# The joint down stage of a DiT block: a normal and a seven-product pair interleaved block by block, and an eighth pair with seven products

## The chip, the cores and the metric

One NeuronCore of one Trainium2 chip runs the whole program in one launch. The metric is the device time of that launch in microseconds; lower is better. A core has engines that run their own instruction streams: TensorE (PE, with its weight loads PEld), VectorE (DVE), ScalarE (ACT), GpSimd (POOL) and SyncE (SP, which here only issues DMAs). They wait for one another by semaphores.

## The reference, cut to what matters

```python
D_MODEL = 2048; SEQ = 256
D_FF = 256 * ((8 * D_MODEL // 3 + 255) // 256)          # 5632
...
def conv_ffn(h, w_up, conv_w, conv_b, w_down):
    a, u = jnp.split(h @ w_up, 2, axis=-1)
    return (jax.nn.silu(depthwise_conv(a, conv_w, conv_b)) * u) @ w_down
...
        ffn_x = conv_ffn(modulate(x_mid, norm2_g[l], mod_x[:, 3], mod_x[:, 4]), w_up[l], conv_w[l], conv_b[l], w_down[l])
        new_x = x_mid + mod_x[:, 5][:, None, :] * ffn_x
```

Everything is float32. The change touches only the last product, `(...) @ w_down`: 256 tokens by 5632 features times 5632 by 2048.

## The kernel before

A float32 product is made of three matmuls in float32r (`mm3`, line 71): both operands are split into a high part (`hi`, a rounded copy) and a low part (`lo`, the rest), and hi·hi, hi·lo and lo·hi are added up in PSUM. The activations are split once when they are made. The weights come from HBM as 128x1024 tiles (`raw`), and for each tile ACT writes `whi` (a cast, line 143) and DVE writes `wlo` (a subtraction, line 144). `chunk` does that for one tile of the down stage, and `fetch` is its DMA, issued by SP. The pools have four buffers of `raw`, two of `araw`, and three of `whi` and of `wlo`. So the cast of a tile can start only when TensorE has finished with the tile three places ahead of it in program order.

The features are 44 tiles of 128. The gated activations of the first 32 are kept (`g0`, `g1`), and `down_two` multiplies them in one joint stage; the last twelve follow later. The joint stage works in two halves of 1024 output columns (`half`, called twice), and each half walks over 16 pairs of feature tiles. A pair is a 2x2 by 2x2 block product: two feature tiles by two token tiles on one side, two feature tiles by two blocks of 512 columns on the other. A **normal** pair takes eight products of 128x512, in two weight tiles: the rows w21, w22 (`nb` below) and then w11, w12 (`na`). A **seven-product** pair takes Winograd's form with seven products. It needs sums of weights and of activations: weight tile `sb` (w21, w22) gives two products, `sa` (its half w11) one, `t` (two sums, made by `two` on DVE into `araw`) two, and `f` (two more sums, by `four`) two. The sums of activations (s1, s2, s4) are made by `seven_acts` while the up stage runs, and kept in the tiles `sa` and `sb` of SBUF. Each of these groups is one `chunk`, with a cast and a subtraction of its own. Seven pairs, the odd ones up to 13, are of the second kind (`SEVEN`).

Pair follows pair: block i is pair 2i, normal (nb, na), then pair 2i+1 with seven products (sb, sa, t, f). Pairs 14 and 15 are both normal. In each half four PSUM banks (`norm`) take the normal products and some of the seven, and four (`sev`) the rest of them. After the last seven-product pair (line 1003) five instructions combine the `sev` banks into `y`, and at the end of the half four more add the `norm` banks (line 1013). In the second half `before()` calls `turn` (line 1015) after the first pair: 16 transposes on TensorE of the first half's `y`, and eight additions into `xm` on DVE.

Instructions are written in program order, but a scheduler puts each engine's list in an order by priority, and `chunk` raises the priority of its loads and splits, so that they stand ahead of the products that use them. Each engine then runs its own list strictly in that order.

Of the kernel before, what the change touches and what calls it, by code (L numbers as in the profile page):

```python
# [35 lines left out]
SEVEN = (1, 3, 5, 7, 9, 11, 13)  # L36
# [15 lines left out]
def block_kernel(ctx, tc, xct, prm, cst, ada2, wst, out):  # L52
# [895 lines left out]
    def half(n, g0, g1, norm, sev, y, before):  # L948
# [5 lines left out]
        def add(b, a, w, start=False, stop=False):  # L954
            mm3(b, *a, *w, start, stop)
        first = SEVEN[0]
        for p in range(16):
            k1, k2 = 2 * p, 2 * p + 1
            rb, (w21, w22) = chunk(2, fetch)
            a11, a21, a12, a22 = act(k1, 0), act(k1, 1), act(k2, 0), act(k2, 1)  # L960
            if p not in SEVEN:
                st0, sp = p == 0, p == 15
                if sp:
                    ra, (w11, w12) = chunk(2, fetch)
                    for b, u1, u2, v1, v2 in ((0, a11, a12, w11, w21), (1, a11, a12, w12, w22), (2, a21, a22, w11, w21),
                                              (3, a21, a22, w12, w22)):
                        add(norm[b], u1, v1)
                        add(norm[b], u2, v2, stop=True)
                    break
                add(norm[0], a12, w21, st0)  # L970
                add(norm[2], a22, w21, st0)
                add(norm[1], a12, w22, st0)
                add(norm[3], a22, w22, st0)
                ra, (w11, w12) = chunk(2, fetch)
                add(norm[0], a11, w11)
                add(norm[2], a21, w11)
                add(norm[1], a11, w12)
                add(norm[3], a21, w12)
                if p == 0:
                    before()  # L980
                continue
            f, l = p == first, p == SEVEN[-1]
            d = sums[p]
            s1, s2, s4 = [(d[:, 0, i * P:i * P + P], d[:, 1, i * P:i * P + P]) for i in range(3)]
# [9 lines left out]
            add(sev[1], s1, t1, f, l)  # L994
            add(sev[3], a21, t3, f, l)
# [5 lines left out]
            add(sev[2], s2, t2, f, l)  # L1001
# [225 lines left out]
```

## Time and profile before

| | us |
|---|---|
| median of 3 runs | 1675.78 |
| lowest and highest of them | 1674.80 and 1676.34 |
| the profiled execution, device time | 1675.59 |
| the profiled execution, span from first to last instruction | 1673.8 |
| joint down stage, from its first matmul (1295.89) to the first of the next up stage (1468.41) | 172.52 |
| granted clock of TensorE, mean | 1.00 |

The profile is of one execution, and its times are counted from the first instruction. A matmul of 128x512 is listed with 0.39 us, but matmuls overlap, so the distance between two starts tells the rate. In a row of the timeline, what stands in brackets is the time for which the engine stood idle ahead of the instruction, and whose work ended that.

### The profile page before, as it was taken

How to read it: one execution, taken by the hardware profiler on the slowest of the kernel's cores; microseconds unless marked ns; L12 is line 12 of the kernel's file. 1: busy time of each engine (PE TensorE's matmuls, PEld its weight loads, DVE VectorE, ACT ScalarE, POOL GpSimd, SP SyncE). 2: the span in 40 equal slices, each digit the busy share in tenths (PEclk: the TensorE clock that was granted, in tenths of full speed). 3: DMA queues.
4: the chain of work that ended last, by engine and by line, in shares of the span. 5: the costliest groups of instructions: out<-in, count | busy, mean ns of one | idle time of the engine just before them, and what ended most of it. 6: DMA issues, size and time to landing. Idle time of an engine off the chain costs nothing.

```text
span 1673.8 us, 25069 instructions
## 1 busy us (share of the span) xinstructions
PE 1660.3 (99%) x9508; PEld 1392.2 (83%) x9508; DVE 1264.6 (76%) x2014; ACT 862.1 (52%) x1323; POOL 68.3 (4%) x132
## 2 busy tenths in 40 slices
PE   8999999999999999999999999999999999999999
PEld 3668888888888888888888988888888777788887
DVE  3448985666879886878879887788767888866665
ACT  4337542433646764554455665555555555545542
POOL 0000100000000000001100000000000000000000
PEclk9999999999999999999999999999999999999999
DMA  9997834534466657878856577677555565655554
GB/s 378 408 356 246 286 122 158 178 111 154 162 216 211 214 202 277 285 242 280 285 202 234 182 247 256 212 273 252 191 183 190 185 212 187 201 183 192 187 199 149
DMA packets 104153, 371.85 MB, mean 222 GB/s; under 512 B 11488, under 2 KB 13920, under 8 KB 104032
## 3 DMA queue, kind: packets, MB, share of 16 engines
q1 hardware_dynamic: 85600, 303.14, 51.3%
q0 software_dynamic: 18432, 67.12, 12.3%
q8 instruction: 74, 1.21, 0.3%
q14 instruction: 47, 0.39, 0.1%
HBM read 368.11 MB, written 2.10 MB: 221 GB/s over the span
## 4 chain that ended last, share of the span: by engine, by line
PE 96%; DMA 2%; DVE 1%; ACT 0%; issue 0%; SPq 0%; DVEq 0%; ACTq 0%
PE bankm L69 85%; PE banks L69 9%; DMA ringv<-in_wst_dram 1%; DMA ringq<-in_wst_dram 1%; PE banks L406 0%; PE banks L610 0%; PE banks L779 0%; PE banks L602 0%; DVE wlo L114 0%; DMA xraw<-in_xct_dram 0%; PE banks L611 0%; PE banks L224 0%; PE banks L632 0%; PE banks L749 0%; PE banks L1022 0%
## 5 line engine op out<-in xcount | busy, mean ns | idle before, releaser
L69 PE MATMUL bankm<-hl,whi 128*128 128x512 f32 (+1 forms) x3136 | 970.4, 392 | 0.0
L114 DVE TENSOR_TENSOR wlo<-raw,whi 128x1024 fp32r<-128x1024 f32 (+2 forms) x434 | 528.1, 1218 | 240.0 <-ACT whi L113 238.2
L113 ACT CAST whi<-raw 128x1024 fp32r<-128x1024 f32 (+2 forms) x434 | 453.2, 1045 | 479.5 <-PE bankm L69 366.4
L69 PEld LDWEIGHTS bankm<-hl,wlo 128*128 128x128 f32 x2848 | 533.2, 188 | 120.6 <-DVE wlo L114 0.4
L69 PE MATMUL bankm<-hl,wlo 128*128 128x256 f32 (+2 forms) x2848 | 610.2, 287 | 0.0
L69 PEld LDWEIGHTS bankm<-hl,whi 128*128 128x128 f32 x3136 | 494.9, 189 | 20.3 <-DVE hl L153 0.4
L69 PE MATMUL bankm<-whi,hl 128*128 128x512 f32 x640 | 209.2, 395 | 1.2 <-ACT hl L245 1.0
L398 DVE SCALAR_TENSOR_TENSOR acc<-araw,csil,acc 128x1024 f32<-128x1024 f32 x120 | 153.4, 1279 | 2.1 <-DMA araw<-in_ada_dram 1.6
L69 PEld LDWEIGHTS bankm<-whi,hl 128*128 128x128 f32 x640 | 119.7, 188 | 28.0 <-ACT hl L245 2.6
L69 PE MATMUL bankm<-wlo,hl 128*128 128x512 f32 x320 | 124.7, 392 | 0.0
L393 POOL DMA_DIRECT2D araw<-in_ada_dram x128 | 68.1, 532 | 1092.2 <-DVE acc L398 566.9
L143 ACT CAST whi<-raw 128x1024 fp32r<-128x1024 f32 x64 | 61.1, 956 | 42.1 <-PE bankm L69 25.4
L69 PE MATMUL bankm<-yb,whi 128*128 128x512 f32 x256 | 80.7, 397 | 0.0
L144 DVE TENSOR_TENSOR wlo<-raw,whi 128x1024 fp32r<-128x1024 f32 x64 | 69.3, 1104 | 2.2 <-ACT whi L143 1.1
L69 PEld LDWEIGHTS bankm<-wlo,hl 128*128 128x128 f32 x320 | 60.1, 188 | 12.9 <-DVE wlo L144 0.4
L69 PEld LDWEIGHTS bankm<-yb,wlo 128*128 128x128 f32 x256 | 48.1, 188 | 11.3
L910 ACT ACTIVATE fs<-fs,prm 128x256 f32<-128x256 f32 x44 | 26.4, 601 | 49.8 <-DVE fs L464 49.8
L69 PE MATMUL bankm<-yb,wlo 128*128 128x256 f32 x256 | 50.6, 279 | 0.0
L143 ACT CAST whi<-araw 128x1024 fp32r<-128x1024 f32 x28 | 29.5, 1054 | 34.3 <-PE banks L69 17.0
L144 DVE TENSOR_TENSOR wlo<-araw,whi 128x1024 fp32r<-128x1024 f32 x28 | 34.3, 1224 | 16.2 <-ACT whi L143 14.5
L69 PE MATMUL bankm<-whi,g 128*128 128x512 f32 x136 | 46.1, 390 | 0.0
L226 DVE TENSOR_REDUCE tn<-banks 128x8 f32<-128x32 f32 (+1 forms) x9 | 1.7, 188 | 53.1 <-ACT whi L113 50.1
(281 smaller groups left out, 1538.9 us busy)
## 6 DMA issues: line engine op xcount, KB each, us to landing
raw<-in_wst_dram SPq DMA_DIRECT2D x489, 512.0 KB, 4.1
araw<-in_ada_dram POOLq DMA_DIRECT2D x128, 512.0 KB, 4.7
ringv<-in_wst_dram SPq DMA_DIRECT2D x24, 512.0 KB, 9.9
ringq<-in_wst_dram SPq DMA_DIRECT2D x20, 512.0 KB, 9.9
araw<-in_wst_dram SPq DMA_DIRECT2D x10, 512.0 KB, 9.9
xraw<-in_xct_dram SPq DMA_DIRECT2D x8, 512.0 KB, 7.3
raw<-in_wst_dram SPq DMA_DIRECT2D x7, 384.0 KB, 9.9
ringkT<-in_wst_dram SPq DMA_DIRECT2D x5, 512.0 KB, 9.9
```

The source lines that it names most:

```text
L69: return PE.matmul(o, l, r, start=start, stop=stop, skip_group_check=True)
L113: S.copy(hi, raw)
L114: self.last = V.tensor_tensor(lo, raw, hi.bitcast(F32), op=ALU.subtract)
L143: S.copy(hi[:, w], raw[:, w])
L144: V.tensor_tensor(lo[:, w], raw[:, w], hi[:, w].bitcast(F32), op=ALU.subtract)
L226: V.tensor_reduce(m8, aps[:, 0:w].rearrange("p (q g c) -> p q c g", q=2 * n, g=4)[:, :, 0:2, :], axis=AX.X, op=ALU.add)
L393: nc.gpsimd.dma_start(raw, ada2[idx])
L398: V.scalar_tensor_tensor(acc, raw, csil[:, kt, 0:1], acc, op0=ALU.mult, op1=ALU.add)
L910: S.activation(t, s, AF.Identity, bias=cb[:, f:f + 1], scale=cw[:, f, 1:2])
```

## The change

`SEVEN` gets pair 15 as an eighth seven-product pair, and `half` is written in eight blocks. Blocks 0 to 6 hold a normal pair 2i and a seven-product pair 2i+1 whose chunks are mixed: sb, nb, sa, t, na, f (in block 0 nb comes first, and `before()` right behind it). Block 7 holds pair 15, then the combination of the `sev` banks, and then pair 14 as the normal pair that closes the half. The weights are laid out in HBM in the new order. The kept sums grow by 3 KB a partition, and the scratch of GpSimd's DMA descriptors is set from 8192 to 4096.

```diff
-SEVEN = (1, 3, 5, 7, 9, 11, 13)
+SEVEN = (1, 3, 5, 7, 9, 11, 13, 15)
...
-            sums["b"] = big.tile([P, 2, 2, 3 * P], F32R, name="sb", tag="sb")
+            sums["b"] = big.tile([P, 3, 2, 3 * P], F32R, name="sb", tag="sb")
...
-        for p in range(16):
...
+        for i in range(8):
+            pn, ps = (2 * i, 2 * i + 1) if i < 7 else (14, 15)
+            st0, last = i == 0, i == 7
...
+            def normal_b():
+                _, (w21, w22) = chunk(2, fetch)
+                for b, x, w in ((0, n12, w21), (2, n22, w21), (1, n12, w22), (3, n22, w22)):
+                    add(norm[b], x, w, st0)
+
+            def normal_a():
+                _, (w11, w12) = chunk(2, fetch)
+                for b, x, w in ((0, n11, w11), (2, n21, w11), (1, n11, w12), (3, n21, w12)):
+                    add(norm[b], x, w)
+
+            if st0:
+                normal_b()
+                before()
             rb, (w21, w22) = chunk(2, fetch)
...
             add(norm[0], a12, w21)
             add(norm[1], s4, w22)
+            if not st0 and not last:
+                normal_b()
             ra, (w11,) = chunk(1, fetch)
-            add(sev[0], a11, w11, f, l)
+            add(sev[0], a11, w11, st0, last)
...
             r2, (t1, t3) = chunk(2, two, "araw")
...
+            if not last:
+                normal_a()
...
             r4, (t2, t4) = chunk(2, four, "araw")
...
+        y12, y34 = y
+        S.copy(y12[:, 0], sev[0])
...
+        _, (w21, w22) = chunk(2, fetch)
+        _, (w11, w12) = chunk(2, fetch)
+        for b, u1, u2, v1, v2 in ((0, n11, n12, w11, w21), (1, n11, n12, w12, w22), (2, n21, n22, w11, w21),
+                                  (3, n21, n22, w12, w22)):
+            add(norm[b], u1, v1)
+            add(norm[b], u2, v2, stop=True)
...
-    nc = bacc.Bacc("TRN2", target_bir_lowering=False, num_devices=1, dynamic_dma_scratch_size=8192)
+    nc = bacc.Bacc("TRN2", target_bir_lowering=False, num_devices=1, dynamic_dma_scratch_size=4096)
```

What the scheduler makes of it is seen in the engines' lists. First TensorE's list before, in block 0 of the first half: `whi_12180` is sb, `whi_12192` is sa and `whi_12201` is t, whose buffer was that of na. The rows stand right behind the last matmul of na and end with the first that needs t's low part.

```order
L69 MATMUL bankm_12134<-whi_12180,hl_88 128x512
L69 MATMUL bankm_12134<-wlo_12181,hl_88 128x512
L69 MATMUL bankm_12134<-whi_12180,hl_88 128x512
L69 MATMUL bankm_12135<-whi_12180,sa_9137 128x512
L69 MATMUL bankm_12135<-wlo_12181,sa_9137 128x512
L69 MATMUL bankm_12135<-whi_12180,sa_9137 128x512
L69 MATMUL bankm_12133<-whi_12192,hl_88 128x512
L69 MATMUL bankm_12133<-wlo_12193,hl_88 128x512
L69 MATMUL bankm_12133<-whi_12192,hl_88 128x512
L69 MATMUL banks_12138<-whi_12201,sa_9137 128x512
L69 MATMUL banks_12140<-whi_12201,hl_88 128x512
L69 MATMUL banks_12138<-wlo_12202,sa_9137 128x512
```

So the twelfth matmul behind na is the first to need t's low part, and the other blocks are alike. The same place of the changed kernel: `whi_12171` is sb, and `whi_12192` is t, whose buffer was that of nb; the rows stand right behind the last matmul of nb.

```order
L69 MATMUL bankm_12143<-whi_12171,hl_88 128x512
L69 MATMUL bankm_12143<-wlo_12172,hl_88 128x512
L69 MATMUL bankm_12143<-whi_12171,hl_88 128x512
L69 MATMUL bankm_12144<-whi_12171,sa_9137 128x512
L69 MATMUL bankm_12144<-wlo_12172,sa_9137 128x512
L69 MATMUL bankm_12144<-whi_12171,sa_9137 128x512
L69 MATMUL banks_12147<-whi_12192,sa_9137 128x512
L69 MATMUL banks_12149<-whi_12192,hl_88 128x512
L69 MATMUL banks_12147<-wlo_12193,sa_9137 128x512
```

In block 0 it is now the ninth. In a later block of the changed kernel (here block 2 of the first half: `whi_12349` is sa, `whi_12358` t, `whi_12371` na) the chunk that takes over the buffer of nb is na, and the rows again stand right behind the last matmul of nb.

```order
L69 MATMUL bankm_12142<-whi_12349,hl_88 128x512
L69 MATMUL bankm_12142<-wlo_12350,hl_88 128x512
L69 MATMUL bankm_12142<-whi_12349,hl_88 128x512
L69 MATMUL banks_12147<-whi_12358,sa_9137 128x512
L69 MATMUL banks_12147<-wlo_12359,sa_9137 128x512
L69 MATMUL banks_12147<-whi_12358,sa_9137 128x512
L69 MATMUL banks_12149<-whi_12358,hl_88 128x512
L69 MATMUL banks_12149<-wlo_12359,hl_88 128x512
L69 MATMUL banks_12149<-whi_12358,hl_88 128x512
L69 MATMUL bankm_12143<-whi_12371,hl_88 128x512
L69 MATMUL bankm_12145<-whi_12371,hl_88 128x512
L69 MATMUL bankm_12143<-wlo_12372,hl_88 128x512
```

There it is the twelfth again, as before, with na in the place of t. The second place is TensorE's list in the second half, right behind the transposes. Before, `whi_12876` is sb, `whi_12888` sa, `whi_12897` t and `whi_12910` f; na stands ahead of the transposes.

```order
L1022 MATMUL bankm_12812<-cst_77,yva_12142 128x128
L69 MATMUL bankm_12805<-whi_12876,hl_88 128x512
L69 MATMUL bankm_12805<-wlo_12877,hl_88 128x512
L69 MATMUL bankm_12805<-whi_12876,hl_88 128x512
L69 MATMUL banks_12806<-whi_12876,sa_9137 128x512
L69 MATMUL banks_12806<-wlo_12877,sa_9137 128x512
L69 MATMUL banks_12806<-whi_12876,sa_9137 128x512
L69 MATMUL bankm_12809<-whi_12888,hl_88 128x512
L69 MATMUL bankm_12809<-wlo_12889,hl_88 128x512
L69 MATMUL bankm_12809<-whi_12888,hl_88 128x512
L69 MATMUL bankm_12810<-whi_12897,sa_9137 128x512
```

Now `whi_12878` is sb and `whi_12912` is na, which takes over the buffer of sb.

```order
L1024 MATMUL bankm_12832<-cst_77,yva_12151 128x128
L69 MATMUL bankm_12825<-whi_12878,hl_88 128x512
L69 MATMUL bankm_12825<-wlo_12879,hl_88 128x512
L69 MATMUL bankm_12825<-whi_12878,hl_88 128x512
L69 MATMUL banks_12826<-whi_12878,sa_9137 128x512
L69 MATMUL banks_12826<-wlo_12879,sa_9137 128x512
L69 MATMUL banks_12826<-whi_12878,sa_9137 128x512
L69 MATMUL bankm_12825<-whi_12912,hl_88 128x512
L69 MATMUL banks_12827<-whi_12912,hl_88 128x512
L69 MATMUL banks_12826<-whi_12912,hl_88 128x512
L69 MATMUL banks_12828<-whi_12912,hl_88 128x512
L69 MATMUL bankm_12825<-wlo_12913,hl_88 128x512
```

No matmul stands any more between the last of sb and the first of the chunk that takes its buffer. The third place is DVE's list in block 3 of the first half. Before, the low parts are those of nb, na and sb, then sa (512 wide), t and f, with the sums in `araw` between them.

```order
L144 TENSOR_TENSOR wlo_12394<-raw_12392,whi_12393 128x1024
L144 TENSOR_TENSOR wlo_12412<-raw_12410,whi_12411 128x1024
L144 TENSOR_TENSOR wlo_12430<-raw_12428,whi_12429 128x1024
L991 TENSOR_TENSOR araw_12449<-raw_12440 128x512
L992 TENSOR_TENSOR araw_12449<-raw_12440,raw_12428 128x512
L144 TENSOR_TENSOR wlo_12442<-raw_12440,whi_12441 128x512
L998 TENSOR_TENSOR araw_12462<-araw_12449,raw_12428 128x512
L999 TENSOR_TENSOR araw_12462<-araw_12462,raw_12428 128x512
L144 TENSOR_TENSOR wlo_12451<-araw_12449,whi_12450 128x1024
L144 TENSOR_TENSOR wlo_12464<-araw_12462,whi_12463 128x1024
```

Now they are sb, then three sums, nb, sa, the fourth sum, t, na and f.

```order
L144 TENSOR_TENSOR wlo_12403<-raw_12401,whi_12402 128x1024
L986 TENSOR_TENSOR araw_12440<-raw_12431 128x512
L987 TENSOR_TENSOR araw_12440<-raw_12431,raw_12401 128x512
L995 TENSOR_TENSOR araw_12471<-araw_12440,raw_12401 128x512
L144 TENSOR_TENSOR wlo_12415<-raw_12413,whi_12414 128x1024
L144 TENSOR_TENSOR wlo_12433<-raw_12431,whi_12432 128x512
L996 TENSOR_TENSOR araw_12471<-araw_12471,raw_12401 128x512
L144 TENSOR_TENSOR wlo_12442<-araw_12440,whi_12441 128x1024
L144 TENSOR_TENSOR wlo_12455<-raw_12453,whi_12454 128x1024
L144 TENSOR_TENSOR wlo_12473<-araw_12471,whi_12472 128x1024
```

The ten instructions of a block are the same in kind and number; three sums now stand between the low parts of sb and of nb.

## Rows read from the trace of the kernel before

**Rows 1.** The page: span, busy time of each engine, and the chain's shares.

```profile
span 1673.8 us, 25069 instructions
...
PE 1660.3 (99%) x9508; PEld 1392.2 (83%) x9508; DVE 1264.6 (76%) x2014; ACT 862.1 (52%) x1323; POOL 68.3 (4%) x132
...
PE 96%; DMA 2%; DVE 1%; ACT 0%; issue 0%; SPq 0%; DVEq 0%; ACTq 0%
```

**Rows 2.** Busy time by windows: length, PE, PEld, DVE, ACT, POOL; clock, DMA.

```profile
1295.89:1314.52 18.63, 18.63 (x82) 14.68 (x80) 15.75 (x22) 11.38 (x16) 0.00 (x0) 1.00 0.54 177
1314.52:1367.05 52.53, 52.53 (x227) 41.36 (x226) 45.27 (x50) 28.98 (x32) 0.00 (x0) 1.00 0.63 203
1367.05:1401.23 34.18, 33.95 (x155) 27.15 (x154) 30.74 (x40) 16.01 (x19) 0.00 (x0) 1.00 0.52 181
1401.23:1453.71 52.48, 52.48 (x226) 41.31 (x226) 45.27 (x50) 28.92 (x32) 0.00 (x0) 1.00 0.62 204
1453.71:1468.41 14.70, 14.70 (x72) 12.05 (x71) 12.54 (x15) 7.45 (x9) 0.00 (x0) 1.00 0.57 193
```

**Rows 3.** Who waited for whom, 1285 to 1480: total us, times, longest.

```profile
ACT whi L143 <- PE bankm L69: 38.4, 38, 3.7
...
PEld bankm L69 <- DVE wlo L144: 2.6, 7, 0.4
PEld banks L69 <- DVE wlo L144: 2.6, 7, 0.4
```

**Rows 4.** Timeline of block 2, first half: start, us, engine, instruction.

```profile
1322.17 0.62 PE L69 MATMUL bankm<-whi,hl 128*128 128x512 f32 x2
...
1322.64 1.05 ACT L143 CAST whi<-araw 128x1024 fp32r<-128x1024 f32 x1 [2.14 <-DVE araw L999]
...
1323.73 2.59 DVE L144 TENSOR_TENSOR wlo<-araw,whi 128x1024 fp32r<-128x1024 f32 x2 [1.15 <-ACT whi L143]
...
1324.67 0.39 PE L69 MATMUL banks<-whi,hl 128*128 128x512 f32 x1
...
1325.01 0.19 PEld L69 LDWEIGHTS banks<-wlo,sa 128*128 128x128 f32 x1 [0.38 <-DVE wlo L144]
...
1325.35 0.40 PE L69 MATMUL banks<-whi,sa 128*128 128x512 f32 x1
```

**Rows 5.** Groups of instructions, 1312 to 1382, shapes apart: busy, mean ns.

```profile
L144 DVE TENSOR_TENSOR wlo<-raw,whi 128x1024 fp32r<-128x1024 f32 x20 | 23.9, 1220 | 1.3 <-ACT whi L143 0.8
L143 ACT CAST whi<-raw 128x1024 fp32r<-128x1024 f32 x22 | 23.0, 1050 | 10.0 <-PE bankm L69 8.8 <-PE banks L69 1.2
...
L999 DVE TENSOR_TENSOR araw<-araw,raw 128x512 f32<-128x512 f32 x6 | 4.1, 692 | 0.2
```

**Rows 6.** Timeline of DVE around the second half's start.

```profile
1369.97 2.35 DVE L144 TENSOR_TENSOR wlo<-raw,whi 128x1024 fp32r<-128x1024 f32 x2
...
1377.33 1.28 DVE L1013 TENSOR_TENSOR ykT<-bankm,ykT 128x512 f32<-128x512 f32 x2
...
1388.60 1.66 DVE L1025 SCALAR_TENSOR_TENSOR xm<-bankm,modv,xm 128x256 f32<-128x256 f32 x4
```

**Rows 7.** Timeline of PE around the second half's start.

```profile
1386.03 0.28 PE L1022 MATMUL bankm<-cst,ykT 128*128 128x128 f32 x1
...
1387.70 0.47 PE L69 MATMUL bankm<-whi,hl 128*128 128x512 f32 x1
...
1390.84 0.39 PE L69 MATMUL banks<-whi,hl 128*128 128x512 f32 x1
1391.46 0.50 PE L69 MATMUL bankm<-whi,hl 128*128 128x512 f32 x1 [0.23 <-ACT whi L143]
1391.79 0.39 PE L69 MATMUL banks<-whi,hl 128*128 128x512 f32 x1
```

**Rows 8.** Instructions that make a pair's sums (min/median/max ns), 980 to 1262.

```profile
L937 DVE TENSOR_TENSOR t<-fs x7: 282/284/292, 990.7 to 1257.7; 128x128 f32<-128x128 f32 x7
...
L153 DVE TENSOR_TENSOR sb<-t,sb x2: 551/552/553, 1214.8 to 1260.3; 128x384 fp32r<-128x384 f32 x2
```

**Rows 9.** What GpSimd's DMA issues waited for, and who waited for them.

```profile
  DVE acc L398: 566.9, 100
...
  DVE acc L398: 1.6, 1
```

More of the change, by code (lines that the diff above doesn't have):

```diff
@@ L955, in add @@
             mm3(b, *a, *w, start, stop)
-        first = SEVEN[0]
-        for p in range(16):
-            k1, k2 = 2 * p, 2 * p + 1
-            rb, (w21, w22) = chunk(2, fetch)
[L960 to L984, printed above, removed]
@@ new lines, in half @@
+        for i in range(8):
+            pn, ps = (2 * i, 2 * i + 1) if i < 7 else (14, 15)
+            st0, last = i == 0, i == 7
+            a11, a21, a12, a22 = act(2 * ps, 0), act(2 * ps, 1), act(2 * ps + 1, 0), act(2 * ps + 1, 1)
+            n11, n21, n12, n22 = act(2 * pn, 0), act(2 * pn, 1), act(2 * pn + 1, 0), act(2 * pn + 1, 1)
+            d = sums[ps]
+            s1, s2, s4 = [(d[:, 0, i * P:i * P + P], d[:, 1, i * P:i * P + P]) for i in range(3)]
+            def normal_b():
[9 more added lines that the diff above has]
+                before()
+            rb, (w21, w22) = chunk(2, fetch)
@@ L993, in half @@
             r2, (t1, t3) = chunk(2, two, "araw")
-            add(sev[1], s1, t1, f, l)
-            add(sev[3], a21, t3, f, l)
+            add(sev[1], s1, t1, st0, last)
+            add(sev[3], a21, t3, st0, last)
+            if not last:
+                normal_a()
             def four(raw):
@@ L1000, in half @@
             r4, (t2, t4) = chunk(2, four, "araw")
[L1001 removed]
+            add(sev[2], s2, t2, st0, last)
             add(norm[2], a22, t4)
[L1003 to L1009 removed]
+        y12, y34 = y
+        S.copy(y12[:, 0], sev[0])
+        V.tensor_tensor(y34[:, 0], sev[2], y12[:, 0], op=ALU.subtract)
+        V.tensor_tensor(y12[:, 1], sev[1], y34[:, 0], op=ALU.add)
+        V.tensor_tensor(y34[:, 0], sev[3], y34[:, 0], op=ALU.add)
+        V.tensor_tensor(y34[:, 1], sev[3], y12[:, 1], op=ALU.add)
+        _, (w21, w22) = chunk(2, fetch)
[4 more added lines that the diff above has]
+            add(norm[b], u2, v2, stop=True)
         with tc.high_priority(offset=RUSH):
@@ L1209, in downs @@
         return np.concatenate([_duos(np, d[:KT - 2]), _halves(np, d[KT - 2:])], 0)
-    pairs = g["w_down"][0].reshape(NFF // 2, 2, P, 2, 1024)[:16, ::-1].transpose(3, 0, 1, 2, 4).reshape(-1, P, 1024)
+    pairs = g["w_down"][0].reshape(NFF // 2, 2, P, 2, 1024)[:16].transpose(3, 0, 1, 2, 4)
+    order = [(0, 1), (1, 1), (1, 0), (0, 0)]
+    for i in range(1, 7):
+        order += [(2 * i + 1, 1), (2 * i, 1), (2 * i + 1, 0), (2 * i, 0)]
+    order += [(15, 1), (15, 0), (14, 1), (14, 0)]
+    pairs = np.stack([pairs[h, p, k] for h in range(2) for p, k in order])
     parts += [ups(0), ups(1), pairs, ups(2), downs(2)]
```

7 lines of the change are left out of this document (removed).

## The prediction

> **What bounds the kernel now.** I read the page first. PE is busy for 99% of the span and holds 96% of the chain [rows 1], so the stage of the change has to be read on PE. The windows over the joint down stage say the same at first sight: in 52.53 us PE is busy for all 52.53, at granted clock 1.00 [rows 2]. But a matmul of 0.39 us overlaps the next, and a short wait disappears in that overlap, so I went from busy time to distances between starts.
>
> In the timeline eleven steps lie between 1322.17 and 1324.67 [rows 4]: 0.2273 us for a matmul of 128x512. The stage holds 726 of them (two halves of 121 products, three matmuls each). Between the window edges stand 80, 225, 138, 225 and 58, since a block of two pairs has 45 and each edge is the same matmul of a block; 16 transposes fall into the third window and 12 into the last, at 0.104 us each (16 in 1386.03 to 1387.70 [rows 7]). What a window has beyond that is waiting: 18.63 − 18.18 = 0.45; 52.53 − 51.14 = 1.39; 34.18 − 31.37 − 1.66 = 1.15; 52.48 − 51.14 = 1.34; 14.70 − 13.18 − 1.25 = 0.27 [rows 2]. Together 4.60 us. Nothing done to waiting can win more here.
>
> What is waited for stands in the next two views. ACT's casts wait for PE to free a buffer, 38.4 us in 38 waits, and PE's weight loads wait for low parts, 14 times and never over 0.4 us [rows 3]. The timeline has one such case step by step [rows 4]: PE starts the last matmul that reads a buffer at 1322.17, the cast into it starts at 1322.64 (+0.47) and takes 1.05, the low part 1.22 [rows 5] (the second of the two merged on DVE at 1323.73), and the weight load of t's low part starts at 1325.01, after 0.38 of waiting. So **from the last use of a buffer to the use of the next low part in it takes 2.84 us**, whatever else goes on; the high part alone is usable after 0.47 + 1.05 + about 0.06 = 1.58. With 12 slots as cover (2.73 us), 0.11 of the 2.84 is left over, and the restart costs 0.11 more, because the weight load is no longer hidden (1325.01 to 1325.35 is 0.34 against 0.227). That is 0.22, and windows 2 and 4 give 1.39/5 = 0.28 and 1.34/5 = 0.27 a block. Thirteen such blocks are about 3.5 of the 4.60 us; the other 1.1 lies mostly around the half boundary.
>
> The repeating gap has a rule in the Trainium skill, page "Perfetto Trace Analysis", section Optimization Strategy: one gap that keeps repeating on the engine that should be full can mean too few buffers for the next tile. The casts that wait for PE, 38.4 us, agree [rows 3].
>
> **The change, part by part.**
>
> *One pair with seven products instead of eight.* In each half three matmuls fewer: 6 × 0.2273 = **−1.36 us**, on the path. The same section's neighbour in the skill, Identifying the Most-Contended Engine, holds matmul busy time to be a poor measure of how near the limit a kernel is and wants the weight loads' share instead. The rows agree: PE is full in window 2, its weight loads are 41.36 of 52.53, or 79% [rows 2]. By PE's busy time the sum would end at −1.36; by the gaps it goes on, as follows.
>
> *The steady blocks* (2 to 6 of the first half, 1 to 6 of the second: eleven). Three buffers rotate over six chunks, so each chunk takes the buffer of the one three ahead, and what counts is how many slots lie between that one's last matmul and the new low part's first. Before, the tightest was t behind na, 12 slots. Now t has moved to safety (behind sb: nb and sa, 15 slots), but na follows nb with sa 3, t 6 and two high products of its own: 3 + 6 + 2 = 11 matmuls, the low part twelfth. **The same 12 slots, so the same 0.27**: 11 × 0.27 = 2.97 us. nb behind the last na has f 6, sb 6 and its own two, 14 slots or 3.18 us; that covers 2.84. On DVE the block is just as full: from the end of nb's low part, ten slots (2.33) to the release of its buffer, cast 0.47 + 1.05, then na, f and sb's low parts at 1.14 each (two merged in 2.35, so the second begins 1.14 after the first [rows 6]), three sums at 0.60 [rows 6], and nb again 1.22: 10.3 us, against 45 × 0.2273 + 0.22 = 10.45 on PE. It fits with 0.1 us to spare.
>
> *Block 0, first half.* t now stands behind nb with 9 slots, not 12: 2.84 − 2.05 + 0.11 = 0.90.
>
> *Block 1, first half.* Pair 15's sums are made on DVE as the stage begins, four subtractions of 0.28 and a split of 0.55 [rows 8], some 1.5 us with start-up, in a list that has 0.1 us to spare. Cover: the up stage's last loads. I take the 12-slot wait, 0.27, and 0.4 of backlog: 0.67; between 0, if the cover takes all, and 1.2.
>
> *Block 7 of each half.* Pair 15 and the last normal pair have no chunk between them to fill time: f follows with 6 slots, na likewise, then the first chunk of the next stage. Casts that should be hidden for 1.58 have 1.36 of cover and the restart: 1.58 − 1.36 + 0.11 = 0.33, twice, and 0.22 behind it: 0.88 for each half. Bounds 0.4 (one such wait; before, 0.23 in the one case shown, 1391.46 [rows 7]) and 1.3 (all three with a low part that is late as well).
>
> *The second half's start.* The sevens' banks hold the transposes until DVE has added them into `xm`, and the list puts na right behind sb, whose buffer it takes. One slot of cover: 1.58 − 0.23 + 0.11 = **1.46**, and then na's low part, 2.84 behind the release, some 0.4; f's low part stands behind the eight additions on DVE (four in 1.66 [rows 6]), 0.44; nb of block 1 follows with 0.23. Together 2.53; between 1.46 (only the first, the rest absorbed) and 4.0 (f's low part behind all eight, 3.3, less what PE has queued). Before, the transposes were followed by sb, sa and t, all loaded long ago, and the same place waited 0.23 [rows 7].
>
> *The combination of the sevens' banks.* Moved ahead of pair 14, five instructions on ACT and DVE; before, the last eight additions of 1.28 for two [rows 6] stood there too. Hidden behind pair 14's 24 matmuls (5.5 us); without that cover about 3 us. Zero.
>
> *The scratch.* GpSimd issues the earlier stages' loads. Its issues wait for DVE to free the tile (566.9 us, 100 times), and DVE waited for them once, 1.6 us [rows 9]. Half the room may make issues later; the cover is that GpSimd has the tile's whole time. Zero; at most twice that one wait, 3.2.
>
> *DMA.* As many loads as before, in another order, each issued when a `raw` is freed; DMA is busy for 0.52 to 0.63 [rows 2]. Zero.
>
> **Sum.** Waits after: 0.90 + 0.67 + 5 × 0.27 + 0.88 + 2.53 + 6 × 0.27 + 0.88 = 8.83 us. Less 4.60: +4.23. Less 1.36: **+2.87**. The profiled execution took 1675.59 us (span 1673.8 [rows 1], 1.8 around it), 0.19 below the median; 1675.59 + 2.87 = 1678.46, forecast **1678.5 us**.
>
> **The rivals.**
>
> *The mixing hides the waits altogether.* Then 4.60 and 1.36 go: 1669.6. For it: no chunk of the second kind stands next to another of its kind, and 21% of the weight loader's time is free. Against it: na's 12 slots. The skill's section Optimization Strategy says that interleaving stretches with different limits may help. What the rows show is one limit, a buffer three chunks old, on both sides. 7%.
>
> *Only the eleven steady waits go*, if na's cast or low part is faster to start than t's was (t needed a sum by DVE, na only a load). Then 1678.46 − 2.97 = 1675.5. For it: `whi` is the same, but DVE has no sum to do ahead of the cast. Against: in rows 4 the cast waited for the buffer, with the sum just done. 13%.
>
> *The waits stay 4.60 in all, in other places*, and only the matmul count tells: 1674.2. For it: PE full in each window. Against: one slot of cover behind sb. 12%.
>
> *DVE becomes the bound of the block* (the further loss). The loop has 0.1 us to spare; if DVE's dependent steps cost more than the 1.14 and 0.60 counted, from 0.1 a block on, nb's low part is late too, a second wait of about 0.25 in eleven blocks: 1678.46 + 2.75 = 1681.2. For it: 45.27 of 52.53 us on DVE [rows 2], and three sums that now stand in one lump between sb and nb. 18%.
>
> *The scratch costs*: 1678.46 + 3.2 = 1681.7. 4%.
>
> **How the numbers follow.** The forecast has 46%, with 1676.5 to 1680.5 as its own range: the lower bounds give 0.67 + 0.48 × 2 + 1.07 = 2.7 less, the upper 0.5 + 0.42 × 2 + 1.5 = 2.8 more; not all at once, so some 2 each way. Faster or slower by 0.2%, 3.4 us, is about what a measurement can tell from no change: below 1672.4 or above 1679.1. Faster: the first rival (7%) and a corner of the second: 9%. Slower: the last two (22%) and about a third of the forecast's own range: 38%. The rest, 53%, lies within. The range reaches from 1673.5, which takes in the rival of the matmul count, to 1682.0, which takes in DVE's and the scratch's.
>
> **What would show it.** The windows of the stage should add up to 174 to 177 us and not 172.5, and a steady block stay at 10.5 from block to block; if it is 10.2, the second rival is right, if 10.7, DVE's. PE should wait for ACT's cast, over 1.2 us, behind the first sb of the second half, and the first t-low matmul of the stage about 0.9. In block 7 weight loads should wait for casts, not only for low parts. GpSimd's first 1000 us should be the same within 1 us; if the difference lies there, the scratch is the cause. I would be most wrong if PE worked ahead of its list in a way that hides 1.46 us behind sb, or if ACT's cast began before the last matmul on its buffer had started.

## The result and the profile after

The changed kernel takes 1678.99 us (median of 22 runs, 1677.2 to 1681.13), the kernel before 1676.28 (22 runs, 1674.8 to 1677.41): a ratio of 1.0018 with a 95% interval of 1.0011 to 1.0024. The forecast was 1678.5, in a range of 1673.5 to 1682.0. The profiled execution took 1678.05 us, 2.46 more than that of before. First the page:

```profile
span 1676.3 us, 25085 instructions
...
PE 1660.1 (99%) x9502; PEld 1391.1 (83%) x9502; DVE 1271.4 (76%) x2032; ACT 866.2 (52%) x1329; POOL 68.4 (4%) x132
...
PE 93%; DVE 3%; DMA 3%; ACT 1%; issue 0%; SPq 0%; ACTq 0%; DVEq 0%
```

PE's busy time is the same as in [rows 1], and its share of the chain has fallen from 96% to 93%: waiting has come in. To place it I took the same ACT instruction of the up stage ahead of the joint stage and of the up stage behind it. Timelines of ACT, first of the kernel before, then of the changed kernel:

```profile
1287.44 0.60 ACT L910 ACTIVATE fs<-fs,prm 128x256 f32<-128x256 f32 x1 [1.36 <-DVE fs L464]
...
1482.75 0.60 ACT L910 ACTIVATE fs<-fs,prm 128x256 f32<-128x256 f32 x1 [1.36 <-DVE fs L464]
```

```profile
1286.88 0.60 ACT L910 ACTIVATE fs<-fs,prm 128x256 f32<-128x256 f32 x1 [1.36 <-DVE fs L464]
...
1485.19 0.60 ACT L910 ACTIVATE fs<-fs,prm 128x256 f32<-128x256 f32 x1 [1.36 <-DVE fs L464]
```

From 195.31 us the distance has grown to 198.31, so the joint stage is **3.00 us longer**; that the earlier instruction starts 0.56 us sooner comes from the program's first 150 us and stays the same from there on. The prediction said +2.87 for this stage. With 1.36 us of matmuls less, its waits are 4.60 + 1.36 + 3.00 = 8.96 us; 8.83 were forecast.

Windows of the stage (columns as in [rows 2]); the edges are the first matmul and the matmuls that take na's low part in block 2 and in block 6 of the first half and in blocks 1 and 6 of the second:

```profile
1295.34:1323.69 28.35, 27.77 (x121) 21.91 (x120) 24.79 (x37) 17.89 (x24) 0.00 (x0) 1.00 0.54 184
1323.69:1366.32 42.63, 42.25 (x182) 33.27 (x181) 35.56 (x41) 23.17 (x25) 0.00 (x0) 1.00 0.55 193
1366.32:1402.41 36.09, 34.53 (x152) 26.32 (x152) 34.69 (x47) 17.68 (x20) 0.00 (x0) 1.00 0.50 170
1402.41:1454.57 52.16, 52.16 (x226) 41.68 (x225) 44.32 (x51) 29.03 (x31) 0.00 (x0) 1.00 0.58 208
```

Between these edges stand 119, 180, 135 (and 16 transposes) and 225 matmuls. At 0.2273 and 0.104 us each that leaves 28.35 − 27.05 = 1.30, 42.63 − 40.91 = 1.72, 36.09 − 32.35 = 3.74 and 52.16 − 51.14 = 1.02 us of waiting, and, by difference from 8.96, 1.18 for what follows. Forecast, by the same edges: 1.84, 1.08, 3.68, 1.35 and 0.88. A steady block of the second half now takes 10.43 us; before, it took 10.50 [rows 2].

The places themselves, on PE's timeline: block 0 with t's low part, block 7 of the first half, and the second half behind its first sb.

```profile
1299.76 0.40 PE L69 MATMUL banks<-whi,hl 128*128 128x512 f32 x1
1300.68 0.50 PE L69 MATMUL banks<-wlo,sa 128*128 128x512 f32 x1 [0.53 <-DVE wlo L144]
...
1372.35 0.39 PE L69 MATMUL banks<-whi,g 128*128 128x512 f32 x1
1372.88 0.50 PE L69 MATMUL banks<-whi,sb 128*128 128x512 f32 x1
...
1375.06 1.59 PE L69 MATMUL bankm<-whi,g 128*128 128x512 f32 x5
1376.59 0.50 PE L69 MATMUL bankm<-whi,hl 128*128 128x512 f32 x1
...
1386.89 0.40 PE L69 MATMUL banks<-whi,sa 128*128 128x512 f32 x1
1388.47 0.50 PE L69 MATMUL bankm<-whi,hl 128*128 128x512 f32 x1 [1.18 <-ACT whi L143]
1388.81 0.87 PE L69 MATMUL banks<-whi,hl 128*128 128x512 f32 x3
1389.73 0.50 PE L69 MATMUL bankm<-wlo,hl 128*128 128x512 f32 x1
```

By starts, and less 0.2273 for each matmul in between: 0.69 and then a restart of 0.11 in block 0, where the matmul ahead of these (1299.42) already took 0.10 more than 0.2273; 0.30 and 0.39 in block 7, a restart of 0.11 behind each; 1.35 in the second half, 0.11, then 0.24 ahead of the low part. Next, what two casts of block 7 and the one of f in the second half waited for, on ACT, and f's low part in the second half, on DVE:

```profile
1371.78 1.05 ACT L143 CAST whi<-araw 128x1024 fp32r<-128x1024 f32 x1 [0.40 <-DVE araw L996]
...
1374.35 2.19 ACT L143 CAST whi<-raw 128x1024 fp32r<-128x1024 f32 x2
...
1391.47 1.05 ACT L143 CAST whi<-araw 128x1024 fp32r<-128x1024 f32 x1 [3.05 <-PE bankm L69]
```

```profile
1392.55 1.23 DVE L144 TENSOR_TENSOR wlo<-araw,whi 128x1024 fp32r<-128x1024 f32 x1 [0.52 <-ACT whi L143]
```

In block 7 PE waits three times for a cast. f's cast (1371.78) starts behind DVE's fourth sum, but only 0.1 us after its buffer comes free: sb's last matmul starts at 1371.21, and 0.47 [rows 4] behind that is 1371.68. The other two casts (1374.35 and 1375.48) start 0.43 us behind the start of the last matmul on their buffers, which are those of t and of f. In the second half f's low part comes late because f's cast waits for a buffer; DVE stands idle for that cast.

Who was waited for has changed too (the view of [rows 3], 1285 to 1480). PE's weight loads wait longer for low parts than before, and more for casts (0.9 us in 2 waits before, on the same line):

```profile
ACT whi L143 <- PE bankm L69: 37.2, 28, 4.7
ACT whi L143 <- PE banks L69: 29.5, 26, 1.9
...
PEld bankm L69 <- DVE wlo L144: 6.3, 17, 0.8
...
PEld bankm L69 <- ACT whi L143: 3.9, 6, 1.6
```

One wait was not in the forecast. In block 3 of the first half PE stood 0.53 us (by starts) for nb's low part, and the timelines of ACT, DVE and PE's weight loads lead back to a load:

```profile
1334.46 1.05 ACT L143 CAST whi<-raw 128x1024 fp32r<-128x1024 f32 x1 [0.69 <-DMA raw<-in_wst_dram]
...
1336.94 0.69 DVE L986 TENSOR_TENSOR araw<-raw 128x512 f32<-128x512 f32 x1 [0.17 <-DMA raw<-in_wst_dram]
...
1338.76 1.82 DVE L144 TENSOR_TENSOR wlo<-raw,whi 128x1024 fp32r<-128x1024 f32 x2
...
1340.03 0.19 PEld L69 LDWEIGHTS bankm<-wlo,g 128*128 128x128 f32 x1 [0.80 <-DVE wlo L144]
```

sb's load landed late, its cast waited, and DVE came to nb's low part only at 1338.76, behind three sums, of which the first waits 0.17 us for a load itself.

### The profile page after: what moved, and what is told of

Its sections match the earlier page's. It is cut to its first block, busy times and chain, and to the rows that moved or that the text cites. A ratio compares the mean times of both kernels' runs of the same rounds, so it can differ in the third digit from the quotient of the medians.

```text
span 1676.3 us, 25085 instructions
## 1 busy us (share of the span) xinstructions
PE 1660.1 (99%) x9502; PEld 1391.1 (83%) x9502; DVE 1271.4 (76%) x2032; ACT 866.2 (52%) x1329; POOL 68.4 (4%) x132
## 4 chain that ended last, share of the span: by engine, by line
PE 93%; DVE 3%; DMA 3%; ACT 1%; issue 0%; SPq 0%; ACTq 0%; DVEq 0%
PE bankm L69 82%; PE banks L69 8%; DVE wlo L144 1%; DMA ringv<-in_wst_dram 1%; ACT whi L143 1%; DMA ringq<-in_wst_dram 1%; PE banks L406 0%; PE banks L610 0%; DMA raw<-in_wst_dram 0%; PE banks L779 0%; PE banks L602 0%; DVE wlo L114 0%; DMA xraw<-in_xct_dram 0%; PE banks L611 0%; DVE araw L995 0%
## 5 line engine op out<-in xcount | busy, mean ns | idle before, releaser
L143 ACT CAST whi<-raw 128x1024 fp32r<-128x1024 f32 (+1 forms) x64 | 60.3, 945 | 57.1 <-PE bankm L69 28.4
L144 DVE TENSOR_TENSOR wlo<-raw,whi 128x1024 fp32r<-128x1024 f32 (+1 forms) x64 | 68.4, 1086 | 16.3 <-ACT whi L143 16.1
L143 ACT CAST whi<-araw 128x1024 fp32r<-128x1024 f32 x32 | 33.7, 1053 | 19.6 <-PE bankm L69 8.9
L144 DVE TENSOR_TENSOR wlo<-araw,whi 128x1024 fp32r<-128x1024 f32 x32 | 39.1, 1221 | 2.2 <-ACT whi L143 1.2
```

The source lines that it names most:

```text
L143: S.copy(hi[:, w], raw[:, w])
L144: V.tensor_tensor(lo[:, w], raw[:, w], hi[:, w].bitcast(F32), op=ALU.subtract)
```

## The experiments

**Theory**: what counts is how many matmul slots lie between the release of a `whi`/`wlo` buffer and the use of what comes into it (2.84 us, some 13 slots). **Main rival**: DVE, whose list has no room in the blocks. Each kernel was timed against the kernel before in five rounds. "Stage" is the distance between the two ACT rows used above; before it is 195.31 us, in the changed kernel 198.31. Where an edit changes the order of the loads, the order of the weights in HBM follows it; those lines are left out of the cuts.

| run | median us | before | ratio, 95% interval | stage against before, us |
|---|---|---|---|---|
| changed kernel | 1678.99 | 1676.28 | 1.0018 (1.0011 to 1.0024) | +3.00 |
| e1 block 0 in the old order | 1677.96 | 1676.35 | 1.0011 (1.0002 to 1.0021) | +2.15 |
| e2 na ahead of t | 1681.63 | 1676.35 | 1.0035 (1.0022 to 1.0047) | +5.08 |
| e3 eighth pair, no mixing | 1681.22 | 1676.35 | 1.0031 (1.0019 to 1.0044) | +4.64 |
| e4 four buffers everywhere | 1674.97 | 1676.35 | 0.9995 (0.9986 to 1.0003) | −3.97 |
| e5 mixing, seven pairs | 1676.15 | 1676.48 | 1.0000 (0.9991 to 1.0009) | −0.22 |
| e6 block 7 mixed too | 1680.20 | 1676.48 | 1.0022 (1.0013 to 1.0031) | +4.99 |
| e7 as e2, six raw | 1678.79 | 1676.48 | 1.0014 (1.0005 to 1.0022) | +2.13 |
| e8 changed, four buffers in the stage | 1673.13 | 1676.48 | 0.9982 (0.9973 to 0.9990) | −2.89 |
| e9 scratch alone | 1676.62 | 1676.44 | 1.0001 (0.9992 to 1.0009) | +0.13 |
| e10 changed, six raw | 1677.70 | 1676.44 | 1.0009 (1.0001 to 1.0018) | +1.59 |
| e11 before, four buffers in the stage | 1672.68 | 1676.44 | 0.9978 (0.9969 to 0.9987) | −4.31 |
| e12 eight pairs, no mixing, four buffers | 1674.73 | 1676.44 | 0.9991 (0.9982 to 1.0000) | −2.35 |

**e1, block 0 in the old order.**

```diff
             if st0:
                 normal_b()
+                normal_a()
                 before()
...
-            if not last:
+            if not st0 and not last:
                 normal_a()
```

> The changed kernel with block 0 in the order of before (nb, na, before(), sb, sa, t, f); blocks 1 to 7 stay as changed. Theory (cover by slots): block 0 of the first half has t's low part 12 slots behind instead of 9, so 0.25 us of waiting and not 0.8, and in the second half na no longer stands right behind sb: about 1.4 us of waiting there instead of 2.4. Together 1.6 us less than the changed kernel, about 1.2 us over the kernel before. Rival (DVE binds in the blocks, so a wait saved at the start is paid later): no gain, still 2.7 to 3.0 us over the kernel before.

The stage lost 0.85 us of its 3.00, half of what was expected. The 1.35 us behind sb is gone; in its place several waits of 0.2 to 0.4 us came at the same start, since the sevens' first products still stand behind the additions into `xm`. By starts block 0 waits some 0.4 us less, but block 1 waits 0.89 us where it waited 0.33, as the rival has it; and the wait of block 3 with its restart, 0.64 us, isn't there in this run, though block 3 is the same. So the edit itself brought little.

**e2, na ahead of t.** In blocks 1 to 6 `normal_a()` stands ahead of the chunk of t; nothing else is changed.

```diff
             add(sev[0], a11, w11, st0, last)
+            if not last and not st0:
+                normal_a()
...
-            if not last:
-                normal_a()
+            if st0:
+                normal_a()
```

> The changed kernel with na ahead of t in blocks 1 to 6 (sb, nb, sa, na, t, f); blocks 0 and 7 stay as changed. Theory (cover by slots): each new low part in blocks 2 to 6 then has at least 13 slots (2.96 us) behind the release of its buffer, where 2.84 are needed; the waits of blocks 1 to 6 go, 0.2 us each and the odd one of 0.6: 2.4 to 3.0 us less than the changed kernel, so 0 to 0.6 over the kernel before. Rival (DVE's chain through the block is the limit): the block stays at 10.4 us, the gain is under 0.5 us, 2.3 or more over the kernel before.

A miss, and on the far side of both: the stage is 2.1 us longer than in the changed kernel. Every low part has its 13 slots, and yet PE waits. Timelines of the place where block 3 of the second half begins, ACT, DVE and then PE:

```profile
1415.13 1.05 ACT L143 CAST whi<-raw 128x1024 fp32r<-128x1024 f32 x1 [1.40 <-issue]
...
1416.64 0.69 DVE L989 TENSOR_TENSOR araw<-raw 128x512 f32<-128x512 f32 x1 [1.47 <-DMA raw<-in_wst_dram]
...
1417.85 2.35 DVE L144 TENSOR_TENSOR wlo<-raw,whi 128x1024 fp32r<-128x1024 f32 x2
...
1419.12 0.50 PE L69 MATMUL bankm<-wlo,hl 128*128 128x512 f32 x1 [1.13 <-DVE wlo L144]
```

DVE stands 1.47 us at a sum (L989) whose load hasn't landed, while sb's low part, whose cast ended at 1416.18, stands behind it. SP's own waits (total us, times, longest), here and then in the changed kernel, show that its issues wait for earlier loads:

```profile
SPq L148 <- DMA raw<-in_wst_dram: 20.9, 11, 2.7
```

```profile
SPq L148 <- DMA raw<-in_wst_dram: 2.6, 4, 1.2
```

The `raw` of sb and of sa is held until the sums are made, and only four exist; e7 asks whether that is the reason.

**e3, the eighth pair without the mixing.**

```diff
-            if st0:
-                normal_b()
+            if not last:
+                normal_b()
+                normal_a()
+            if st0:
                 before()
...
-            if not st0 and not last:
-                normal_b()
...
-            if not last:
-                normal_a()
```

> The eighth seven-product pair without the mixing: blocks 0 to 6 are nb, na, sb, sa, t, f as before, block 7 as in the changed kernel. Theory (cover by slots): 1.36 us of matmuls less than before, 0.27 a steady block as before, the second half's start about 1 us as before, block 7 about 1.0 us a half instead of some 0.2: about 0.1 us over the kernel before, within 0.7 either way. Rival (the eighth pair itself costs, by its sums and DVE's load): 2 us or more over the kernel before.

A miss for the theory's size: +4.64 us, not 0.1. Pair 15 now stands directly behind pair 13, with no normal chunk between, and there most of the time is lost: by starts 2.3 us of waits in block 7 of each half, where the kernel before has none. Another 1.3 us or so more than before stand at the second half's start, with one low part 1.03 us late. Windows of that stretch, of e3 and then of the changed kernel's block 7:

```profile
1367.00:1378.78 11.78, 10.33 (x42) 6.92 (x40) 11.44 (x13) 8.15 (x9) 0.00 (x0) 1.00 0.45 144
```

```profile
1366.32:1377.00 10.68, 10.52 (x44) 7.76 (x43) 10.58 (x13) 6.99 (x8) 0.00 (x0) 1.00 0.57 192
```

DVE is busy for 11.44 of 11.78 us, and for 10.58 of 10.68. A seven-product pair is three low parts of 1.14 [rows 6], one of 0.60 and four sums of 0.60 (from start to start on DVE), 6.4 us of DVE, beside 21 matmuls, 4.77 us of PE. A normal pair is 2.3 us of DVE beside 5.5 of PE. So two pairs of the first kind in a row leave DVE behind; e12 tries that with one more buffer.

**e4, four buffers of whi and of wlo**.

```diff
-            hi, lo = [strm.tile([P, 1024], F32R, name=nm, bufs=3) for nm in ("whi", "wlo")]
+            hi, lo = [strm.tile([P, 1024], F32R, name=nm, bufs=4) for nm in ("whi", "wlo")]
...
```

The stream of the other stages gets its fourth buffers too.

> The changed kernel with four buffers of whi and of wlo instead of three. To make room the pairs 11, 13 and 15 share the sums of the activations of pairs 1, 3 and 5 (a third tile of sums is left out, so part of the result is another; the work is the same). Theory (cover by slots): each new low part has 13 slots or more behind the release of its buffer, so all waits of the steady blocks and of block 7 go; what is left is the start of the second half, 0.8 to 1.5 us. The stage takes 720 x 0.2273 + 28 x 0.104 + about 1.2 = 167.8 us instead of 175.5 in the changed kernel. Rival (DVE binds): the stage stays above 173 us. Other stages may change too, so the stage is read, not the whole.

The stage became 6.97 us shorter than in the changed kernel, where 7.7 were expected: in the steady blocks it is the buffers, and DVE alone doesn't hold them at 10.4 us. The stages ahead of it became slower (the first ACT row comes 5.0 us later than before), so the median is only 1.4 us below the kernel before, not clear of noise (0.9986 to 1.0003).

**e5, the mixing without the eighth pair.** Blocks 0 to 6 as in the change, pairs 14 and 15 normal.

```diff
-SEVEN = (1, 3, 5, 7, 9, 11, 13, 15)
+SEVEN = (1, 3, 5, 7, 9, 11, 13)
...
-        for i in range(8):
+        for i in range(7):
...
```

> The mixing without the eighth pair: blocks 0 to 6 as in the changed kernel, pairs 14 and 15 normal as before. Theory (cover by slots): 1.36 us of matmuls more than the changed kernel; of its 0.9 us of waiting in each block 7 all but 0.1 goes, since four normal chunks of 12 products follow; in the second half na no longer stands right behind sb, so 1.2 us of waiting there and not 2.4. Together about 1.6 us less than the changed kernel, 1.2 over the kernel before. Rival (block 7 costs nothing worth naming, the loss is all in the mixed blocks): 1.36 us more than the changed kernel, 4 over the kernel before.

Better than either: as fast as before. The 1.35 us behind sb isn't there: with seven pairs, sa's matmuls follow sb's on PE's list in the second half, and PE's timeline shows no gap.

```profile
1386.53 0.40 PE L69 MATMUL banks<-whi,sa 128*128 128x512 f32 x1
1386.76 0.39 PE L69 MATMUL bankm<-whi,hl 128*128 128x512 f32 x1
```

So na behind sb comes with the mixing and the eighth pair together. With before, e3 and the changed kernel this makes a square of four: mixing alone −0.22 us, the eighth pair alone +4.64, both +3.00. **What costs time is the eighth pair**; with it, the mixing gives 1.6 us back.

**e6, block 7 mixed too.** Pair 14's rows w21, w22 go in behind sb; w11, w12 close the half.

```diff
-            if not st0 and not last:
+            if not st0:
                 normal_b()
...
```

> The changed kernel with block 7 mixed too (sb, nb, sa, t, f, then the combination, then na); blocks 0 to 6 stay. Theory (cover by slots): f's low part has 12 slots and na 13, so 0.3 us of waiting in block 7 instead of 0.9, and the list of the second half no longer has na right behind sb, though block 1's sb is now the tight one: 1.6 us there instead of 2.4. Together about 2.0 us less than the changed kernel, 0.8 over the kernel before. Rival (the combination of the sevens' banks, about 3.4 us on ACT and DVE, has only 12 matmuls or 2.7 us to hide behind, and the next products wait for the banks): no gain, 2.7 or more over the kernel before.

The rival's sign came true, by another way. In the first half block 7 lost most of its waits, but the additions that close the half, and the sums, then stand together on DVE, and the cast of t stands ahead of na's on ACT. Timelines of ACT and PE, then PE's windows:

```profile
1386.29 1.04 ACT L143 CAST whi<-araw 128x1024 fp32r<-128x1024 f32 x1 [5.44 <-DVE araw L987]
1387.24 1.04 ACT L143 CAST whi<-raw 128x1024 fp32r<-128x1024 f32 x1
...
1388.33 0.51 PE L69 MATMUL bankm<-whi,hl 128*128 128x512 f32 x1 [2.25 <-ACT whi L143]
```

```profile
1386.00:1388.30 2.30, 0.08 (x1) 0.00 (x0) 2.30 (x5) 1.99 (x2) 0.00 (x0) 1.00 0.48 166
1388.30:1390.00 1.70, 1.35 (x4) 0.67 (x4) 1.70 (x3) 0.00 (x0) 0.00 (x0) 0.78 0.77 258
1390.00:1392.50 2.50, 2.40 (x6) 1.92 (x7) 2.40 (x7) 0.00 (x0) 0.00 (x0) 0.50 0.79 274
```

ACT waits 5.44 us for DVE's sum with na's cast behind it, and PE 2.25 us for that cast.

**e7, as e2 with six buffers of raw**, the two more in tiles that are free by then.

```diff
+            n = next(turns) % 6 if extra and tag == "raw" else 0
+            if n > 3:
+                raw = big.tile([P, 1024], F32, name=tag, tag="acc" if n == 4 else "wlx")
...
```

> As e2 (na ahead of t), with six buffers of raw instead of four in the joint stage. Theory (e2 lost because the loads came late: sb's and sa's raw are held until the sums are made, the next load waits for them, and DVE stands in its list at a sum whose load hasn't landed): the waits for late loads go, and with 13 slots of cover those for buffers stay away: 4 to 5 us less than e2, 0 to 0.6 over the kernel before. Rival (it is the order on DVE itself, sums ahead of low parts, whenever the loads land): within 1 us of e2, 4 or more over the kernel before.

Between the two: 2.95 us less than e2 in the stage. SP no longer waits for loads, and DVE's waits for them are down to one of 0.3 us. With six `raw` on both sides this order (+2.13) is 0.5 us behind the changed kernel's own (e10, +1.59), where it was 2.1 behind, so late loads were most of what e2 lost. But a low part still came some 0.18 us late in most blocks: 13 slots leave nothing to spare.

**e8, the changed kernel with a fourth whi and wlo in the joint stage.**

```diff
+            if extra and next(turns) % 4 == 3:
+                hi, lo = [big.tile([P, 1024], F32R, name=nm, tag=t) for nm, t in (("whi", "acc"), ("wlo", "wlx"))]
+            else:
+                hi, lo = [strm.tile([P, 1024], F32R, name=nm, bufs=3) for nm in ("whi", "wlo")]
...
```

> The changed kernel with a fourth buffer of whi and of wlo in the joint stage alone, in room that is free by then; every pair has its own sums, so the output is the reference's. Theory (cover by slots): low parts have 16 slots or more behind the release of their buffer except at the second half's start, so the stage takes 168 us as in e4; the stages ahead of it keep their times: about 7 us less than the changed kernel, 4 less than the kernel before. Rival (what e4 gained in the stage came from the other changes in its lists, such as an earlier start of the loads): less than 3 us gained on the changed kernel.

The stage is 5.89 us shorter than the changed kernel's, 1.1 less than expected; the whole is 3.35 us faster than before, and the early stages are as they were. Of what is left, 0.89 us (by starts) is a wait for a cast near the second half's start, and 0.66 and 0.26 stand in the two blocks 7. The first of these on DVE and PE:

```profile
1363.46 0.69 DVE L992 TENSOR_TENSOR araw<-raw 128x512 f32<-128x512 f32 x1 [1.56 <-DMA raw<-in_wst_dram]
...
1373.70 0.50 PE L69 MATMUL bankm<-wlo,g 128*128 128x512 f32 x1 [0.49 <-DVE wlo L150]
```

A load comes 1.56 us late, and DVE, busy nearly without a gap from there on (9.54 of the next 9.63 us), doesn't catch up before the last low part of pair 14. Four `whi` and `wlo` together with six `raw` were not run.

**e9, the scratch alone.**

```diff
-    nc = bacc.Bacc("TRN2", target_bir_lowering=False, num_devices=1, dynamic_dma_scratch_size=8192)
+    nc = bacc.Bacc("TRN2", target_bir_lowering=False, num_devices=1, dynamic_dma_scratch_size=4096)
```

> The kernel before with the scratch of GpSimd's descriptors set to 4096, nothing else. Theory (GpSimd's issues wait for DVE anyway): the same as before within 0.5 us. Rival (the smaller scratch delays the loads of the early stages): 1 to 3 us over the kernel before, with the joint stage unchanged at 172.5 us.

No difference clear of noise, as the theory said.

**e10, the changed kernel with six raw** (the diff of e7).

> The changed kernel with six buffers of raw in the joint stage; the order stays. Theory (three whi and wlo buffers set the regular waits, late loads only the odd ones): the 0.6 us wait of block 3 and a few tenths like it go, 0.6 to 1.0 us less than the changed kernel; block 7 and the second half's start keep their 0.9 and 2.4 us. Rival (late loads are behind the regular waits too): 2.4 us or more less than the changed kernel.

1.41 us less in the stage: the wait of block 3 is gone, and of block 7's most of the first. The second half's start (1.34 us) and the 0.18 of each steady block stayed. Somewhat more than the theory's 0.6 to 1.0, well short of the rival's 2.4.

**e11, the kernel before with the fourth buffer** (the diff of e8 on the old order).

> The kernel before (seven pairs, no mixing) with the fourth buffer of whi and of wlo in the joint stage, and the scratch at 4096. Theory (cover by slots): every low part has 13 slots or more, so of the 4.6 us of waiting in the joint stage about 0.9 stays, and the kernel is 3.7 us faster than before, 0.4 faster than e8, which has 1.36 us less of matmuls but loses about 2 at the second half's start. Rival (the mixing is what makes the fourth buffer pay): 2 us or less gained.

3.76 us faster than before, and the lowest median of all, though its interval overlaps that of e8. ACT's timeline, the same two instructions as above:

```profile
1289.15 0.60 ACT L916 ACTIVATE fs<-fs,prm 128x256 f32<-128x256 f32 x1 [1.36 <-DVE fs L470]
...
1480.15 0.60 ACT L916 ACTIVATE fs<-fs,prm 128x256 f32<-128x256 f32 x1 [1.36 <-DVE fs L470]
```

191.00 us instead of 195.31: of the 4.60 us of waits 0.3 is left.

**e12, eight pairs without mixing and four buffers** (the diffs of e3 and e8).

> Eight seven-product pairs, no mixing (the order of e3), with the fourth buffer of e8. Theory (cover by slots): block 7 has 16 slots or more and waits no longer; block 1 of the second half still has sb 4 slots behind, some 1.5 us; so 4.6 + 1.36 - 1.8 = 4.2 us faster than before, about 9 faster than e3, and no slower than e8. Rival (with the fourth buffer the mixing still helps): slower than e8 by 1 us or more.

1.71 us faster, not 4.2, and slower than e8 by 1.6: the rival. Block 7 has 16 slots and waits all the same. PE's timeline there, then ACT's, and the window ahead of it:

```profile
1372.86 0.40 PE L69 MATMUL bankm<-whi,g 128*128 128x512 f32 x1
1373.79 0.50 PE L69 MATMUL banks<-wlo,sb 128*128 128x512 f32 x1 [0.53 <-DVE wlo L150]
```

```profile
1371.42 1.05 ACT L149 CAST whi<-araw 128x1024 fp32r<-128x1024 f32 x1 [2.61 <-DVE araw L1000]
```

```profile
1363.43:1371.32 7.89, 7.89 (x36) 6.41 (x35) 7.82 (x10) 3.69 (x4) 0.00 (x0) 1.00 0.47 156
```

DVE is busy for 7.82 of 7.89 us and only then done with the last sum of pair 15. ACT has waited 2.61 us for that sum, with the casts of pair 14 behind it, and the low part that PE waits for comes behind this cast. Against e11 the eighth pair costs 1.96 us though it saves 1.36: 3.3 us of waits, of which by starts 1.5 and 1.1 stand in the two blocks 7, where the slots are enough. That fits DVE's 6.4 us a pair, and the mixed form with four buffers (e8), which has a normal pair between most of them, loses less.

## Why the prediction was right, step by step

The time (1678.5 against 1678.99), the stage (+2.87 against +3.00) and its waits (8.83 against 8.96) came as forecast, from the forecast places in the main. That the sum is so close is in part luck: by the windows above the errors are −0.54, +0.64, +0.06, −0.33 and +0.30 us, and they cancel. The forecast also starts from one execution, 0.69 us under the median of the 22; from median to median the change is +2.71 us.

- *What bounds it*: right. The chain of 2.84 us with three buffers is what makes the steady waits; e8 and e11, which add a buffer and, in e11, set the scratch that e9 found to cost nothing, take 5.89 and 4.31 us out of the stage. In [rows 4] the bracket of the cast names DVE's sum, which ended at the same time as the buffer came free; in blocks 1, 3 and 4 the cast starts just as far behind the last matmul, and the bracket names PE. The Trainium skill, page "Perfetto Trace Analysis", section Optimization Strategy, has a rule for a gap that repeats (it can mean too few buffers). These runs agree, with a gap of 0.27 a block that goes. The Trainium skill, same page, section Identifying the Most-Contended Engine, holds matmul busy time to be a poor measure of how near the limit a kernel is. The two profiles agree: by PE's busy time, 1660.1 us against 1660.3, the changed kernel is no slower, and it is by 2.7 us.
- *−1.36 for the matmuls*: the page counts 9502 matmul records against 9508, six fewer, as worked out.
- *Steady blocks*: right in that the mixing leaves them about as they were (mixing alone, −0.22 us). By size it was 0.20 a block in the second half and not 0.27; in the first half 0.43 on average, of which the 0.53 us of block 3, and a little in others, come from late loads, which were costed at nothing (the item *DMA*). That step failed. e10 shows the loads' part: with six `raw` the wait of block 3 goes. e1 and e6, with the same block 3 and four `raw`, have no wait there either, so it doesn't come in every run.
- *Block 0*: 0.90, with the restarts on both sides, against 0.90. *Block 1*: some 0.33 against 0.67; DVE's backlog was mostly covered.
- *Block 7*: 0.88 was forecast, and 0.91 (first half) and 0.93 (second) are what PE's starts give, for the reason given, the cover of the casts: two of the three casts start when PE frees their buffer, f's 0.1 us later. What the prediction doesn't have is that DVE, busy for 99% of that stretch, is close behind: with the fourth buffer of e8 waits for DVE's low parts stay there, and e12, without the mixing, has the slots and waits all the same.
- *Second half's start*: 1.46 + 0.4 + 0.44 + 0.23 was forecast; PE's rows give 1.35 + 0.11 + 0.24 + 0.11 there and 0.44 at f's low part, some 2.3. The reason given for the 0.44 failed: f's low part doesn't stand behind the additions into `xm`, DVE is idle for 0.52 us ahead of it; f's cast waited for its buffer. That the size came out is luck. Nor is na behind sb the mixing's alone, since e5 hasn't got it; the scheduler's list puts na there only with both edits.
- *The rivals*: DVE as the bound of each block (18%) was refuted for the steady blocks by e4 and e8; in block 7 DVE comes close. Waits that vanish, or stay 4.60 in all, are refuted by the 8.96. "Only the eleven steady waits go" didn't happen. The scratch is refuted by e9.
- *Readings*: the 0.23 us at 1391.46 [rows 7] is PE's idle time; by starts that wait is 0.39 and a restart of 0.11, so that place waited 0.50 us before and not 0.23. Ten slots in DVE's loop are 2.27 us and not 2.33. Neither changes the sum.

What the experiments expected of the orders (e2, e3, e6, e12) went wrong four times, by counting slots for PE and not what stands in DVE's list, and in e2 the loads that this list waits for. That DVE's load is what block 7 waits for once the buffers are enough is worked out from the rows of e8 and e12; no run took work from DVE there to show it by itself. Why the profile of e6 shows a larger loss (+4.99) than its median (+3.7) stays open; its second half has two waits of 0.76 and 0.60 us behind loads that came 0.81 and 0.65 us late, and whether other executions have them isn't known.

## What to carry to other kernels

A product saved by sums is paid on the engine that makes the sums: compare the vector engine's time for such a pair (6.4 us here) with the matrix engine's (4.8), and keep a pair of the other kind between two of them. Where the same short gap stands in every block, count the slots between the release of a buffer and its next use, and try one more buffer ahead of any new order: here it gave 3.8 us, and none of the new orders tried with three buffers gave a gain clear of noise. A wait that a new order removes for one engine is easily put in front of another: read what stands behind each instruction that waits, in the lists of all of them.

## What was not expected of the hardware

In e6 PE ran its 16 transposes (1.8 us) and then stood idle for 2.25 us, and its granted clock then fell from 1.00 to 0.50, the lower level of 1.2 GHz, for the window of 2.5 us from 1390.00 on (0.78 in the one before it). There two starts lie 0.43 us apart instead of 0.2273:

```profile
1391.12 0.63 PE L69 MATMUL banks<-wlo,hl 128*128 128x512 f32 x1
1391.55 0.63 PE L69 MATMUL bankm<-whi,hl 128*128 128x512 f32 x1
```

In the changed kernel six 128x512 matmuls stand between the transposes and an idle time of 1.18 us, and the clock stayed at 1.00. The single wait so cost about 1.2 us more than its length, by the starts up to 1392.76.

The stages ahead of the joint one are the same in all kernels but e4, and yet they end up to 2.5 us apart: the first ACT row stands at 1286.88 in the changed kernel and at 1289.33 in e9, whose median differs from before's by 0.2 us. In these two profiles the difference is there by 150 us and stays. A difference of 1 us between two profiles' spans says little; the distance between two rows around the stage agreed with the medians to about 0.7 us in eleven of the thirteen kernels.
